# Key lookup in a product-key mixture: each chosen index picked on its token's partition by VectorE, or on the pair's partition by TensorE and VectorE

## The chip, the cores and the metric

One core of a Trainium2 chip runs the whole program. The metric is the device time of one execution in microseconds (us), lower is better. The core's engines run side by side and wait for each other through semaphores: TensorE (PE, with its weight loads shown as PEld), VectorE (DVE), ScalarE (ACT), GpSimd (POOL) and SyncE (SP), which issues DMAs. ACT issues DMAs too.

## What is computed

Two transformer blocks, one after the other, on 256 tokens of width 1024. The change lies in the last layer of the second block, a mixture of 16384 single-row experts with product keys:

```python
q = (xb @ w_q).reshape(TOK_BLOCK, PEER_HEADS, 2, PEER_DHALF)          # 256, 8, 2, 128
s = jnp.einsum('thcd,hcnd->thcn', q, sub_keys).astype(jnp.float32)    # 128 scores per list
top_s, top_i = lax.top_k(s, K)                                        # K = 16
cand = top_s[:, :, 0, :, None] + top_s[:, :, 1, None, :]
best_s, best_c = lax.top_k(cand.reshape(TOK_BLOCK, PEER_HEADS, K * K), K)
i1 = jnp.take_along_axis(top_i[:, :, 0], best_c // K, axis=-1)
i2 = jnp.take_along_axis(top_i[:, :, 1], best_c % K, axis=-1)
e = (i1 * PEER_NKEYS + i2).reshape(TOK_BLOCK, PEER_HEADS * K)
gate = jax.nn.softmax(best_s, axis=-1).reshape(TOK_BLOCK, PEER_HEADS * K)
act = jax.nn.gelu(jnp.einsum('td,ted->te', xb, expert_u[e]), approximate=False)
return jnp.einsum('te,ted->td', gate * act, expert_v[e])
```

So every token has 8 heads with two lists of 128 scores. The 16 best of each list are kept, all 256 sums of a pair of lists are formed, the 16 best sums are kept, and each names a place in the first list (its number divided by 16) and one in the second (the remainder). `i1` and `i2` are the keys found at these places.

## The kernel before

**The expert layer as matrix products.** The kernel does not gather expert rows. It forms the activations of all 16384 experts, in 128 chunks of 128, and multiplies them by a dense matrix `G` of gates, which is zero where an expert was not chosen. `act(c)` (line 1887) takes one chunk of `expert_u`: 24 matmuls of 128x256 in float32 parts (each number is a high part plus a low part, three products of eight slices of the width), then a Gelu on ACT (line 1893). The first 90 chunks run before `G` is needed and are parked in DRAM (line 1908).

**The weight stream.** Chunks come through class `Stream`: SP loads a raw chunk (4 buffers), ACT rounds it to the high part (line 362), and DVE or POOL subtracts to get the low part (line 363). Three buffers `hl` hold split chunks, so a chunk can be split only when the one three places ahead of it has been multiplied. Line 658 gives the subtraction to POOL for chunks below `POOLU` (36), and to DVE for the others.

**The choice beside it.** `queries` (line 1717) makes the 16 projections `qT` on PE, splits them (ACT high part, DVE low part), splits the keys `kT` and scores them. `choose` (line 1762) is a generator on DVE: `top16` (line 1751) is five operations (MAX8, FIND_INDEX8, MATCH_REPLACE8, MAX8, FIND_INDEX8) and runs for 16 lists in each of two token tiles, on 128 tokens as partitions. Then for each tile and head one addition makes the 256 sums `cand` (line 1780) and `top16` finds the best of them, values `bv` and numbers `bi`. Line 1786 and 1787 cut `bi` into the two places. The lookup compares each place with 0 to 15 (`eq`, line 1794), multiplies by the list's indices `tf` (line 1796) and sums over the 16 (line 1799): for each tile, side and head two operations of 128x256, so 32 comparisons and 32 products, and 4 sums. After that come the softmax, PE transposes (line 382) that put the 128 pairs (8 heads x 16) on partitions, and copies to `gi` (indices) and `gg` (the gates as a sum of three bf16 numbers, through `left`, lines 1824 to 1829).

**The gates.** `gates` (line 1832) makes 64 groups of four tokens: DVE one-hot tiles `e` and `m`, 12 bf16 matmuls of 128x128 on PE, a copy into `G` by ACT.

**What sets the order.** `first` (line 1905) writes `act(c)`, then takes as many steps of the side generator (`choose`, then `gates`) as its running sum allows: each step yields a number of ns, and the sum stays below `SIDE` (2850) times the chunks so far. Nine steps of `choose` are taken inside `queries`. A scheduler then places instructions on each engine. In `queries` it keeps the written order on DVE and in the first loop of `first` on ACT, but it may still bring other instructions forward into them.

Names: `hl_9657` is a buffer's tile with its number; `pb` are the PSUM tiles of `act` and `queries` (4), `py` those of the side work (4), `raw` the loaded chunks.

Of the kernel before, what the change touches and what calls it, by code (L numbers as in the profile page):

```python
# [29 lines left out]
WP = 400  # L30
EXP_M05 = math.exp(-0.5)
C0 = 90
POOLU = 36
LENT = 3
OUT = 1000
QUAD, PAIR = 150, 20
# [9 lines left out]
SIDE = 2850  # L46
LATE, CH = 6000, 1.0
# [11 lines left out]
def bias_onehot(dist):  # L59
# [6 lines left out]
CONST = {}  # L66
CONST_GROUPS = [["ident"], ["flip", "hpar", "hpair", "maskc"],
                ["mean512", "blk64", "strict", "incl", "lev1", "lev2", "lev4", "lev8", "lev16", "eye32", "ind", "indt"],
                ["iota"]]


def make_consts():
    p = np.arange(128)
    parts = {}
# [2 lines left out]
    parts["mean512"] = np.full((128, 128), 1.0 / 512)  # L77
    parts["blk64"] = (p // 64)[:, None] == (p // 64)[None, :]
    parts["iota"] = np.tile(np.arange(128), (128, 1))
    s64, t64 = (p % 64)[:, None], np.arange(64)[None, :]  # L80
    parts["strict"] = s64 < t64
    parts["incl"] = s64 <= t64
# [258 lines left out]
class Kern:  # L341
# [1419 lines left out]

    def choose(self, tk, sc, gi, gg):

        nc = self.nc
        found = []
        best = [(tk.tile([128, 16, 16], F32, name=f"tv{tt}"), tk.tile([128, 16, 16], U32, name=f"ti{tt}")) for tt in range(2)]
        for g in range(4):
            for tt in range(2):
                for k in range(4 * g, 4 * g + 4):
                    self.top16(tk, sc[tt][:, k], best[tt][0][:, k], best[tt][1][:, k])  # L1770
                    yield 1700 * CH
        for tt in range(2):
            tv, ti = best[tt]
            tf = tk.tile([128, 16, 16], F32, tag="tf", name=self.name("tf"), bufs=1)
            nc.vector.tensor_copy(tf, ti)
            bv = tk.tile([128, 8, 16], F32, tag="bv", name=self.name("bv"), bufs=1)
            bi = tk.tile([128, 8, 16], U32, tag="bi", name=self.name("bi"), bufs=1)
            for h in range(8):
                cand = tk.tile([128, 16, 16], F32, tag="cand", name=self.name("cand"), bufs=2)
                nc.vector.tensor_add(cand, tv[:, 2 * h, :, None].to_broadcast([128, 16, 16]),  # L1780
                                     tv[:, 2 * h + 1, None, :].to_broadcast([128, 16, 16]))
                self.top16(tk, cand.rearrange("p a b -> p (a b)"), bv[:, h], bi[:, h])
                yield 2900 * CH
            rs = []
            ij = [tk.tile([128, 8, 16], U32, tag=f"ij{c}", name=self.name("ij"), bufs=1) for c in range(2)]
            nc.vector.tensor_scalar(ij[0], bi, 4, None, op0=OP.logical_shift_right)
            nc.vector.tensor_scalar(ij[1], bi, 15, None, op0=OP.bitwise_and)
            for c in range(2):
                jf = tk.tile([128, 8, 16], F32, tag="jf", name=self.name("jf"), bufs=2)
                nc.vector.tensor_copy(jf, ij[c])  # L1790
                eq = tk.tile([128, 8, 16, 16], F32, tag="eq", name=self.name("eq"), bufs=1)
                res = tk.tile([128, 8, 16], F32, tag="res", name=self.name("res"), bufs=4)
                for h in range(8):
                    nc.vector.tensor_tensor(eq[:, h], jf[:, h, :, None].to_broadcast([128, 16, 16]),
                                            self.iota[:, None, :16].to_broadcast([128, 16, 16]), op=OP.is_equal)
                    nc.vector.tensor_mul(eq[:, h], eq[:, h], tf[:, 2 * h + c, None, :].to_broadcast([128, 16, 16]))
                    if h % 4 == 3:
                        yield 3400 * CH
                nc.vector.tensor_reduce(res, eq, axis=AX.X, op=OP.add)
                rs.append(res)  # L1800
                yield 2400 * CH
            ev = tk.tile([128, 8, 16], F32, tag="ev", name=self.name("ev"), bufs=2)
            nc.vector.tensor_sub(ev, bv, bv[:, :, 0:1].to_broadcast([128, 8, 16]))
            found.append((rs, ev))
        yield LATE
        sm = tk.tile([128, 2, 8], F32, name="smx")
        for tt, (_, ev) in enumerate(found):
            nc.scalar.activation(ev, ev, AF.Exp)
            nc.vector.tensor_reduce(sm[:, tt], ev, axis=AX.X, op=OP.add)
        nc.vector.reciprocal(sm, sm)  # L1810
        for tt, (_, ev) in enumerate(found):
            nc.vector.tensor_mul(ev, ev, sm[:, tt, :, None].to_broadcast([128, 8, 16]))
        yield 2 * SIDE
        for tt, (rs, ev) in enumerate(found):
            t = slice(tt * 32, tt * 32 + 32)
            p = self.pb()
            for c, x in enumerate((*rs, ev)):
                self.tr(p[:, c * 128:(c + 1) * 128], x.rearrange("p a b -> p (a b)"))
            nc.scalar.activation(gi[:, t].rearrange("p b c t -> p c b t"),
                                 p[:, :256].rearrange("p (c b t) -> p c b t", c=2, t=4), AF.Copy)  # L1820

            part = gg[:, t].rearrange("p b k t -> p k b t")
            src = p[:, 256:384].rearrange("p (b t) -> p b t", t=4)
            for k in range(3):
                nc.scalar.activation(part[:, k], src, AF.Copy)
                if k < 2:
                    left = tk.tile([128, 32, 4], F32, tag="left", name=self.name("left"), bufs=2)
                    nc.vector.tensor_sub(left, src, part[:, k])
                    src = left
        yield 600  # L1830

    def gates(self, gp, G, gi, gg):
# [26 lines left out]
    def peer(self, ctx):  # L1859
        tc, nc, A = self.tc, self.nc, self.A  # L1860
        st = self.st
        pp = ctx.enter_context(tc.tile_pool(name="peer", bufs=1))
        self.wide = ctx.enter_context(tc.tile_pool(name="wide2", bufs=1, space=PSUM))
        self.consts(3, pp)
        self.iota = self.c("iota")
        hT = self.hT
        self.iota2 = pp.tile([128, 128, 2], BF16, name="iota2")
        nc.gpsimd.tensor_copy(self.iota2, self.iota[:, :, None].to_broadcast([128, 128, 2]))
# [4 lines left out]
        tk = tke.enter_context(tc.tile_pool(name="topk", bufs=1))  # L1873
        sc = [tk.tile([128, 16, 128], F32, name=f"sc{tt}") for tt in range(2)]
        choose = self.choose(tk, sc, gi, gg)
        with tc.manual_schedule(engines={mybir.EngineType.DVE}):
            self.queries(tk, hT, sc, choose)
# [40 lines left out]
        with tc.manual_schedule(engines={mybir.EngineType.Activation}):  # L1918
            c = first(0, lambda c: self.G is not None or c == C0)
# [96 lines left out]
```

## Time and profile before

| | |
|---|---|
| three runs | 1550.85, 1552.71, 1559.87 us; median 1552.71 |
| the profiled execution | 1557.66 us, of which its span is 1555.9 us |
| PE busy | 1450.3 us, 93% of the span |
| DVE busy | 1135.2 us, 73% |
| ACT busy | 805.4 us, 52% |
| POOL busy | 271.3 us, 17% |
| expert layer | from about 690 us to the end; first loop from 747 us, `gates` from 930 to 1079 us |

Times within the profile count from the span's start. The clock of TensorE stands in the windows as a share of full speed: 1.00 is 2.4 GHz and 0.50 is 1.2 GHz. An idle time is named by what ended it.

### The profile page before, as it was taken

How to read it: one execution, taken by the hardware profiler on the slowest of the kernel's cores; microseconds unless marked ns; L12 is line 12 of the kernel's file. 1: busy time of each engine (PE TensorE's matmuls, PEld its weight loads, DVE VectorE, ACT ScalarE, POOL GpSimd, SP SyncE). 2: the span in 40 equal slices, each digit the busy share in tenths (PEclk: the TensorE clock that was granted, in tenths of full speed). 3: DMA queues.
4: the chain of work that ended last, by engine and by line, in shares of the span. 5: the costliest groups of instructions: out<-in, count | busy, mean ns of one | idle time of the engine just before them, and what ended most of it. 6: DMA issues, size and time to landing. Idle time of an engine off the chain costs nothing. (4 is left out here: it accounts for less than half of the span.)

```text
span 1555.9 us, 29408 instructions
## 1 busy us (share of the span) xinstructions
PE 1450.3 (93%) x11816; PEld 1321.3 (85%) x11816; DVE 1135.2 (73%) x2036; ACT 805.4 (52%) x1274; POOL 271.3 (17%) x136
## 2 busy tenths in 40 slices
PE   5999999998988789999998399999999999999997
PEld 4989799997877679989998399999999998888886
DVE  6765776778579974957999759987555556776776
ACT  4634565555463445544544167776444445455444
POOL 3100310004353323035786000000000000000000
PEclk9999999999899989999999699999999999999999
DMA  6622455554422211454565274444555557777773
GB/s 212 235 87 82 135 189 179 186 189 168 137 95 84 70 61 69 165 175 160 182 231 197 78 223 150 154 165 164 191 188 187 189 190 253 254 241 242 241 243 129
DMA packets 93024, 263.43 MB, mean 169 GB/s; under 512 B 10271, under 2 KB 34975, under 8 KB 92760
## 3 DMA queue, kind: packets, MB, share of 16 engines
q1 hardware_dynamic: 77200, 243.80, 46.4%
q10 hardware_dynamic: 15688, 17.76, 3.2%
q8 instruction: 92, 1.51, 0.4%
q14 instruction: 44, 0.36, 0.1%
HBM read 247.61 MB, written 13.91 MB: 168 GB/s over the span
## 5 line engine op out<-in xcount | busy, mean ns | idle before, releaser
L370 PE MATMUL pb<-hT,hl 128*128 128x256 f32 (+1 forms) x4944 | 629.6, 286 | 33.9 <-DVE hl L363 30.4
L370 PEld LDWEIGHTS pb<-hT,hl 128*128 128x128 f32 x4944 | 612.7, 193 | 41.4 <-DVE hl L363 30.8
L362 ACT ACTIVATE hl<-raw 128x1024 fp32r<-128x1024 f32 x412 | 434.3, 1054 | 236.9 <-issue 161.4
L363 DVE TENSOR_TENSOR hl<-raw,hl 128x1024 fp32r<-128x1024 f32 (+1 forms) x319 | 391.7, 1229 | 116.6 <-ACT hl L362 116.3
L370 PE MATMUL py<-hl,coef 128*128 128x512 f32 x1536 | 356.8, 390 | 0.8 <-ACT coef L362 0.6
L370 PEld LDWEIGHTS py<-hl,coef 128*128 128x128 f32 x1536 | 285.5, 188 | 60.6 <-ACT coef L362 1.4
L363 POOL TENSOR_TENSOR hl<-raw,hl 128x1024 fp32r<-128x1024 f32 x93 | 229.8, 2475 | 343.1 <-ACT hl L362 227.8
L1893 ACT ACTIVATE act<-pb 128x256 f32<-128x256 f32 x128 | 49.5, 387 | 179.5 <-PE pb L370 179.5
L1972 POOL TENSOR_TENSOR end<-end,end 128x512 f32<-128x512 f32 x2 | 2.6, 1278 | 700.5 <-DVE end L1970 699.0
L370 PE MATMUL py<-hT,hl 128*128 128x272 f32 (+1 forms) x768 | 118.0, 304 | 1.6 <-POOL hl L363 1.6
L370 PEld LDWEIGHTS py<-hT,hl 128*128 128x128 f32 x768 | 103.1, 198 | 8.3 <-issue 4.8
L363 DVE TENSOR_TENSOR coef<-act,coef 128x256 fp32r<-128x256 f32 x128 | 54.1, 423 | 72.4 <-ACT coef L362 72.4
L1897 DVE TENSOR_TENSOR act<-act,G 128x256 f32<-128x256 f32 x128 | 53.8, 421 | 35.4 <-ACT act L1893 33.2
L1246 DVE SCALAR_TENSOR_TENSOR acc<-UU,vt,acc 128x256 f32<-128x256 f32 x120 | 75.7, 673 | 0.7
L1856 ACT ACTIVATE G<-py 128x512 f32<-128x512 f32 x64 | 67.9, 1132 | 8.0 <-PE py L370 7.9
L1843 DVE TENSOR_TENSOR m<-e,gg 128x1536 bf16<-128x1536 bf16 x64 | 60.7, 954 | 0.8
L370 PE MATMUL py<-m,e 128*128 128x128 bf16 x768 | 53.6, 219 | 1.0 <-DVE m L1843 0.8
L362 ACT ACTIVATE coef<-act 128x256 fp32r<-128x256 f32 x128 | 51.6, 404 | 4.5 <-DVE act L1897 4.5
L1839 DVE TENSOR_TENSOR e<-gi,iota 128x1024 bf16<-128x1024 bf16 x64 | 43.6, 687 | 8.8 <-PE py L370 8.7
L370 PEld LDWEIGHTS <-e 128*128 128x128 bf16 x768 | 44.3, 97 | 5.6 <-DVE m L1843 3.0
L370 PE MATMUL py<-hl,gu 128*128 128x512 f32 x192 | 47.4, 393 | 0.3 <-DVE hl L363 0.2
L370 PEld LDWEIGHTS py<-hl,gu 128*128 128x128 f32 x192 | 34.9, 188 | 7.6 <-DVE hl L363 0.5
(408 smaller groups left out, 1424.6 us busy)
## 6 DMA issues: line engine op xcount, KB each, us to landing
raw<-in_ws_dram SPq DMA_DIRECT2D x172, 512.0 KB, 3.4
raw<-in_ut_dram SPq DMA_DIRECT2D x128, 512.0 KB, 3.3
raw<-in_ev_dram SPq DMA_DIRECT2D x128, 512.0 KB, 4.2
ad<-act ACTq DMA_DIRECT2D x90, 128.0 KB, 3.1
act<-ad SPq DMA_DIRECT2D x90, 128.0 KB, 3.1
wf<-fd ACTq DMA_DIRECT2D x2, 800.0 KB, 4.6
x<-in_x_dram SPq DMA_DIRECT2D x2, 512.0 KB, 5.9
xd<-x ACTq DMA_DIRECT2D x1, 1024.0 KB, 4.1
```

The lines of the kernel that those rows point to most:

```text
L362: self.nc.scalar.activation(h, src, AF.Copy)
L363: (eng or self.nc.vector).tensor_sub(l, src, h.bitcast(F32))
L370: self.nc.tensor.matmul(out, lhsT, rhs, start=start, stop=stop, skip_group_check=True)
L1246: nc.vector.scalar_tensor_tensor(acc[:, i], UU[:, i, 16 + j:272 + j], self.v("cw", 4 * j + i), acc[:, i], op0=OP.mult, op1=OP.add)
L1839: nc.vector.tensor_tensor(e.rearrange("p c a i j -> p (c a) i j"), gi[:, b].rearrange("p c (a j) -> p (c a) j", j=2)[:, :, None, :].to_bro ...
L1843: nc.vector.tensor_mul(m, e[:, 0][:, None].to_broadcast([128, 3, 2, 128, 2]), gg[:, b].rearrange("p k (a j) -> p k a j", j=2)[:, :, :, Non ...
L1856: nc.scalar.activation(G[:, :, 4 * b:4 * b + 4].rearrange("p a t -> p t a"), p.rearrange("p (t a) -> p t a", t=4), AF.Copy)
L1893: nc.scalar.activation(a, p[:, :S], AF.Gelu)
L1897: nc.vector.tensor_mul(a, a, self.G[:, c])
L1972: nc.gpsimd.tensor_mul(t[:, tt], x[:, tt, cols[1]], g[:, cols[1]])
```

## The change

It replaces the comparisons, products and sums of the lookup. The places are transposed to pairs on partitions as numbers (`pT`, two sides, 256 tokens), and so are the lists of indices (`tT`, bf16). `sel` is a constant set of 16 matrices, made once from `cst3`: matrix r has a one where row h*16+r meets the 16 columns of head h. `spread` multiplies it with `tT`: each pair's partition receives the index that stands at place r of its head's list. One DVE operation compares the places with r and multiplies with that (`hit`, bf16), and a matmul with the identity (`identb`) adds it into `found`; with r from 0 to 15 and two sides these are 32 spreading matmuls, 32 DVE operations and 32 adding matmuls, all 128x256. The sums `cand` of eight heads become one operation of 128x2048 per tile. Casts go to ACT (`tf`, `pf`). The yields are new, `POOLU` is 38, and `cst3` moves from the pool `peer` to the pool `topk`.

```diff
-POOLU = 36
+POOLU = 38
-                ["iota"]]
+                ["iota", "place"]]
+    parts["place"] = p[:, None] - p[None, :] // 16 * 16
     def choose(self, tk, sc, gi, gg):
...
-                    yield 1700 * CH
+                    yield 1650 * CH
+        bv = [tk.tile([128, 8, 16], F32, name=f"bv{tt}") for tt in range(2)]
+        bi = [tk.tile([128, 8, 16], U32, name=f"bi{tt}") for tt in range(2)]
         for tt in range(2):
...
+            cand = tk.tile([128, 8, 16, 16], F32, tag="cand", name=self.name("cand"), bufs=1)
+            nc.vector.tensor_add(cand, tv[:, 0::2, :, None].to_broadcast([128, 8, 16, 16]),
+                                 tv[:, 1::2, None, :].to_broadcast([128, 8, 16, 16]))
+            yield 2300 * CH
             for h in range(8):
...
-                yield 2900 * CH
...
+                self.top16(tk, cand[:, h].rearrange("p a b -> p (a b)"), bv[tt][:, h], bi[tt][:, h])
+                yield 2400 * CH
+        ev, pl, tf = [], [], []
+        for tt in range(2):
+            x = tk.tile([128, 8, 16], F32, name=f"ev{tt}")
+            nc.vector.tensor_sub(x, bv[tt], bv[tt][:, :, 0:1].to_broadcast([128, 8, 16]))
+            ev.append(x)
+            x = tk.tile([128, 2, 128], U32, name=f"place{tt}")
+            flat_bi = bi[tt].rearrange("p a b -> p (a b)")
+            nc.vector.tensor_scalar(x[:, 0], flat_bi, 4, None, op0=OP.logical_shift_right)
+            nc.vector.tensor_scalar(x[:, 1], flat_bi, 15, None, op0=OP.bitwise_and)
+            pl.append(x)
+            yield 900 * CH
         yield LATE
         sm = tk.tile([128, 2, 8], F32, name="smx")
+        pf = []
+        for tt in range(2):
+            x = tk.tile([128, 2, 8, 16], F32, name=f"tf{tt}")
+            nc.scalar.activation(x.rearrange("p c h r -> p h c r"), best[tt][1].rearrange("p (h c) r -> p h c r", c=2), AF.Copy)
+            tf.append(x)
+            x = tk.tile([128, 2, 128], F32, name=f"pf{tt}")
+            nc.scalar.activation(x, pl[tt], AF.Copy)
+            pf.append(x)
+            nc.scalar.activation(ev[tt], ev[tt], AF.Exp)
...
+        identb = tk.tile([128, 128], BF16, name="identb")
+        nc.scalar.activation(identb, self.ident, AF.Copy)
...
-        yield 2 * SIDE
+        yield SIDE
+        pT = tk.tile([128, 2, 256], F32, name="pT")
+        tT = tk.tile([128, 2, 256], BF16, name="tT")
+        for tt in range(2):
+            p = self.p1()
+            for c in range(2):
+                self.tr(p[:, c * 128:(c + 1) * 128], tf[tt][:, c].rearrange("p h r -> p (h r)"))
+            nc.scalar.activation(tT[:, :, tt * 128:tt * 128 + 128], p[:, :256].rearrange("p (c t) -> p c t", c=2), AF.Copy)
+            p = self.p1()
+            for c, x in enumerate((pf[tt][:, 0], pf[tt][:, 1], ev[tt].rearrange("p a b -> p (a b)"))):
+                self.tr(p[:, c * 128:(c + 1) * 128], x)
+            nc.scalar.activation(pT[:, :, tt * 128:tt * 128 + 128], p[:, :256].rearrange("p (c t) -> p c t", c=2), AF.Copy)
...
+            yield 900
+        found = self.p1()
+
+        def spread(c, r):
+            p = self.p1()
+            for i in range(2):
+                self.mm(p[:, 256 * i:256 * i + 256], self.sel[:, r + i], tT[:, c], True, True)
+            return p
+
+        todo = [(c, r) for c in range(2) for r in range(0, 16, 2)]
+        nxt = spread(*todo[0])
+        for n, (c, r) in enumerate(todo):
+            p = nxt
+            if n + 1 < len(todo):
+                nxt = spread(*todo[n + 1])
+            for i in range(2):
+                w = tk.tile([128, 256], BF16, tag="hit", name=self.name("hit"), bufs=3)
+                nc.vector.scalar_tensor_tensor(w, pT[:, c], float(r + i), p[:, 256 * i:256 * i + 256], op0=OP.is_equal, op1=OP.mult)
+                self.mm(found[:, 256 * c:256 * c + 256], identb, w, r + i == 0, r + i == 15)
+            yield 950 * CH
+        nc.scalar.activation(gi.rearrange("p b c t -> p c b t"), found.rearrange("p (c b t) -> p c b t", c=2, t=4), AF.Copy)
         yield 600
     def peer(self, ctx):
...
-        self.consts(3, pp)
...
+        self.consts(3, tk)
...
+        self.sel = tk.tile([128, 16, 128], BF16, name="sel")
+        nc.vector.tensor_tensor(self.sel, self.c("place")[:, None, :].to_broadcast([128, 16, 128]),
+                                self.c("iota")[:, :16, None].to_broadcast([128, 16, 128]), op=OP.is_equal)
```

Lines after the change stand one lower at first (the split is lines 363 and 364, `act` is line 1922). What the schedule makes of it is shown at three places.

First DVE where `queries` begins, before the change: the low part of a chunk, then the low parts of the queries (`qT`) and of the keys (`kT`).

```order
L363 TENSOR_TENSOR hl_7710<-raw_7416,hl_7710 128x1024
L363 TENSOR_TENSOR qT<-pb_7705,qT 128x256 x2
L363 TENSOR_TENSOR qT<-pb_7750,qT 128x256 x2
L363 TENSOR_TENSOR qT<-pb_7725,qT 128x256
L363 TENSOR_TENSOR qT<-pb_7801,qT 128x256
```

The same place after the change:

```order
L364 TENSOR_TENSOR hl_7710<-raw_7416,hl_7710 128x1024
L1902 TENSOR_TENSOR sel<-cst_7775 128x2048
L364 TENSOR_TENSOR qT<-pb_7705,qT 128x256 x2
L364 TENSOR_TENSOR qT<-pb_7750,qT 128x256 x2
L364 TENSOR_TENSOR qT<-pb_7725,qT 128x256
```

`sel` now stands ahead of the first query. On ACT's queue the DMA of `cst3` moved from ahead of six splits and copies to just ahead of the DMA of the keys (`kr`).

Second, DVE between two projections inside `queries`, before the change: an operation of the first `top16` steps, then the sums of one head, brought forward from later, and the start of their `top16`.

```order
L1760 MAX_INDEX ti_7925<-tv_7924,s_880_7966 128x8
L1780 TENSOR_TENSOR cand_8933<-tv_7924 128x256
L1756 MAX bv_8931<-cand_8933 128x8
L1757 MAX_INDEX bi_8932<-bv_8931,cand_8933 128x8
L1758 MATCH_REPLACE s_998_8935<-bv_8931,cand_8933 128x256
L363 TENSOR_TENSOR qT<-pb_7977,qT 128x256
L363 TENSOR_TENSOR kT<-kr,kT 128x512
```

The same place after the change:

```order
L1760 MAX tv_7926<-s_880_7968 128x8
L1761 MAX_INDEX ti_7927<-tv_7926,s_880_7968 128x8
L364 TENSOR_TENSOR qT<-pb_7979,qT 128x256
L364 TENSOR_TENSOR kT<-kr,kT 128x512
L1757 MAX tv_7926<-sc_7778 128x8
```

The head's sums no longer stand there; a second head's, 27 rows on, are gone in the same way.

Third, ACT after the change, where the lookup begins: `act_9687` is chunk 32, `hl_9737` is the split of chunk 35 and `hl_9797` that of chunk 36.

```order
L1937 DMA ad<-act_9687 128x256
L1820 ACTIVATE tT<-py_9692 128x2x128
L1824 ACTIVATE pT<-py_9696 128x2x128
L1830 ACTIVATE gg<-py_9696 128x32x4
L1830 ACTIVATE gg<-left_9702 128x32x4
L1830 ACTIVATE gg<-left_9705 128x32x4
L1820 ACTIVATE tT<-py_9708 128x2x128
L1824 ACTIVATE pT<-py_9712 128x2x128
L1830 ACTIVATE gg<-py_9712 128x32x4
L1830 ACTIVATE gg<-left_9718 128x32x4
L1830 ACTIVATE gg<-left_9721 128x32x4
L363 ACTIVATE hl_9737<-raw_9543 128x1024
```

The split of chunk 35 stands behind ten copies, four of which wait for DVE. Before the change the corresponding copies stood between splits:

```order
L1819 ACTIVATE gi<-pb_10303 128x2x32x4
L1825 ACTIVATE gg<-pb_10303 128x32x4
L1893 ACTIVATE act_10442<-pb_10417 128x256
L362 ACTIVATE hl_10481<-raw_10228 128x1024
L1825 ACTIVATE gg<-left_10309 128x32x4
```

Two copies, a Gelu and a split stand there before the next copy that waits for DVE.

## Rows read from the trace of the kernel before

**Rows 1.** Who waited for whom, 690 to 1090 us: total us, times, longest.

```profile
PE pb L370 <- DVE hl L363: 29.7, 1, 29.7
...
PE pb L370 <- DVE qT L363: 3.2, 2, 1.9
```

**Rows 2.** Timeline of PE from 745 us: start, length, instructions [idle before <-releaser].

```profile
747.39 102.68 PE L370 MATMUL pb<-hT,hl 128*128 128x256 f32 x866
879.75 36.66 PE L370 MATMUL pb<-hT,hl 128*128 128x256 f32 x286 [29.68 <-DVE hl L363]
...
930.35 0.85 PE L370 MATMUL py<-m,e 128*128 128x128 bf16 x12
931.01 0.36 PE L370 MATMUL pb<-hT,hl 128*128 128x256 f32 x1
```

**Rows 3.** Windows: busy PE, PEld, DVE, ACT, POOL, then clock, DMA share, GB/s.

```profile
820.00:840.00 20.00, 20.00 (x172) 20.00 (x171) 20.00 (x16) 10.26 (x15) 17.62 (x8) 1.00 0.66 234
...
860.00:880.00 20.00, 0.25 (x1) 0.25 (x2) 19.83 (x51) 0.00 (x0) 0.00 (x0) 0.50 0.00 0
```

**Rows 4.** Groups by line, 700 to 930 us; columns: group, count | busy us, mean ns | idle before, releaser.

```profile
L363 POOL TENSOR_TENSOR hl<-raw,hl 128x1024 fp32r<-128x1024 f32 x45 | 110.8, 2463 | 36.5 <-ACT hl L362 36.5
L362 ACT ACTIVATE hl<-raw 128x1024 fp32r<-128x1024 f32 x63 | 66.7, 1059 | 21.5 <-ACT act L1893 21.0 <-DVE hl L363 0.5
L1794 DVE TENSOR_TENSOR eq<-jf,cst 128x256 f32<-128x256 f32 x32 | 29.7, 968 | 0.0
L1796 DVE TENSOR_TENSOR eq<-eq,tf 128x256 f32<-128x256 f32 x32 | 29.7, 968 | 0.0
...
L1780 DVE TENSOR_TENSOR cand<-tv 128x256 f32<-128x256 f32 x16 | 16.9, 1056 | 0.0
...
L1799 DVE TENSOR_REDUCE res<-eq 128x128 f32<-128x2048 f32 x4 | 9.1, 2277 | 0.1
...
L1893 ACT ACT_TABLE_LOAD x2 | 2.6, 1283 | 0.0
...
L1825 ACT ACTIVATE gg<-left 128x128 bf16<-128x128 f32 x4 | 1.2, 308 | 1.3 <-DVE left L1828 1.3
```

**Rows 5.** Timeline of DVE: two lookup pairs, and the end of the choice.

```profile
837.87 2.95 DVE L1794 TENSOR_TENSOR eq<-jf,cst 128x256 f32<-128x256 f32 x2
...
878.49 3.49 DVE L363 TENSOR_TENSOR hl<-raw,hl 128x1024 fp32r<-128x1024 f32 x3
```

**Rows 6.** Line 1794: ns min/median/max, first and last start, form.

```profile
L1794 DVE TENSOR_TENSOR eq<-jf,cst x32: 400/419/2649, 794.6 to 875.2; 128x256 f32<-128x256 f32 x32
```

**Rows 7.** Tile qT: the same columns.

```profile
L363 DVE TENSOR_TENSOR qT<-pb,qT x16: 403/420/426, 699.5 to 745.4; 128x256 fp32r<-128x256 f32 x16
```

**Rows 8.** Groups with shapes apart, whole span.

```profile
L1135 DVE SCALAR_TENSOR_TENSOR cv<-pb,vt,cv 128x254 f32<-128x254 f32 x44 | 21.0, 480 | 1.3
```

**Rows 9.** Timeline of PE, 675 to 745 us.

```profile
675.46 1.03 PE L382 MATMUL pb<-ident,xg 128*128 128x128 f32 x8
...
702.68 3.08 PE L370 MATMUL pb<-hT,hl 128*128 128x256 f32 x24 [1.30 <-DVE qT L363]
...
731.58 2.69 PE L370 MATMUL pb<-kT,qT 128*128 128x128 f32 x13 [1.86 <-DVE qT L363]
734.07 10.86 PE L370 MATMUL pb<-hT,hl 128*128 128x256 f32 x72
```

**Rows 10.** Windows of 2 us: busy PE, clock, DMA share, GB/s.

```profile
732.00:734.00 2.00, 2.00 (x12) 0.50 0.19 64
...
740.00:742.00 2.00, 2.00 (x19) 1.00 0.00 0
```

**Rows 11.** Timelines of ACT and POOL around the queries' start.

```profile
688.86 0.35 ACTq L689 DMA_DIRECT2D cst<-in_cst_dram  x1
...
698.63 0.35 ACTq L1721 DMA_DIRECT2D kr<-in_keys_dram  x1
...
690.76 0.40 POOL L1868 CAST iota<-cst 128x256 bf16<-128x256 f32 x1 [7.71 <-DMA cst<-in_cst_dram]
```

More of the change, by code (lines that the diff above doesn't have):

```diff
@@ L1764, in choose @@
         nc = self.nc
-        found = []
         best = [(tk.tile([128, 16, 16], F32, name=f"tv{tt}"), tk.tile([128, 16, 16], U32, name=f"ti{tt}")) for tt in range(2)]
@@ L1770, in choose @@
                     self.top16(tk, sc[tt][:, k], best[tt][0][:, k], best[tt][1][:, k])
-                    yield 1700 * CH
+                    yield 1650 * CH
+        bv = [tk.tile([128, 8, 16], F32, name=f"bv{tt}") for tt in range(2)]
+        bi = [tk.tile([128, 8, 16], U32, name=f"bi{tt}") for tt in range(2)]
         for tt in range(2):
-            tv, ti = best[tt]
-            tf = tk.tile([128, 16, 16], F32, tag="tf", name=self.name("tf"), bufs=1)
-            nc.vector.tensor_copy(tf, ti)
@@ L1776, in choose @@
-            bv = tk.tile([128, 8, 16], F32, tag="bv", name=self.name("bv"), bufs=1)
-            bi = tk.tile([128, 8, 16], U32, tag="bi", name=self.name("bi"), bufs=1)
-            for h in range(8):
[L1779 to L1782, printed above, removed]
-                yield 2900 * CH
@@ L1784, in choose @@
[L1784 to L1800, printed above, removed]
-                yield 2400 * CH
@@ L1802, in choose @@
-            ev = tk.tile([128, 8, 16], F32, tag="ev", name=self.name("ev"), bufs=2)
-            nc.vector.tensor_sub(ev, bv, bv[:, :, 0:1].to_broadcast([128, 8, 16]))
-            found.append((rs, ev))
+            tv, _ = best[tt]
+            cand = tk.tile([128, 8, 16, 16], F32, tag="cand", name=self.name("cand"), bufs=1)
+            nc.vector.tensor_add(cand, tv[:, 0::2, :, None].to_broadcast([128, 8, 16, 16]),
+                                 tv[:, 1::2, None, :].to_broadcast([128, 8, 16, 16]))
@@ L1805, in choose @@
         yield LATE
         sm = tk.tile([128, 2, 8], F32, name="smx")
-        for tt, (_, ev) in enumerate(found):
-            nc.scalar.activation(ev, ev, AF.Exp)
-            nc.vector.tensor_reduce(sm[:, tt], ev, axis=AX.X, op=OP.add)
-        nc.vector.reciprocal(sm, sm)
-        for tt, (_, ev) in enumerate(found):
-            nc.vector.tensor_mul(ev, ev, sm[:, tt, :, None].to_broadcast([128, 8, 16]))
-        yield 2 * SIDE
-        for tt, (rs, ev) in enumerate(found):
-            t = slice(tt * 32, tt * 32 + 32)
[L1816 to L1820, printed above, removed]
+        pf = []
@@ new lines, in choose @@
+        for tt in range(2):
[6 more added lines that the diff above has]
+            nc.scalar.activation(ev[tt], ev[tt], AF.Exp)
+            nc.vector.tensor_reduce(sm[:, tt], ev[tt], axis=AX.X, op=OP.add)
@@ new lines, in choose @@
+        identb = tk.tile([128, 128], BF16, name="identb")
+        nc.scalar.activation(identb, self.ident, AF.Copy)
+        nc.vector.reciprocal(sm, sm)
+        for tt in range(2):
+            nc.vector.tensor_mul(ev[tt], ev[tt], sm[:, tt, :, None].to_broadcast([128, 8, 16]))
+        yield SIDE
+        pT = tk.tile([128, 2, 256], F32, name="pT")
+        tT = tk.tile([128, 2, 256], BF16, name="tT")
+        for tt in range(2):
+            p = self.p1()
[6 more added lines that the diff above has]
+            nc.scalar.activation(pT[:, :, tt * 128:tt * 128 + 128], p[:, :256].rearrange("p (c t) -> p c t", c=2), AF.Copy)
+            t = slice(tt * 32, tt * 32 + 32)
@@ L1863, in peer @@
         self.wide = ctx.enter_context(tc.tile_pool(name="wide2", bufs=1, space=PSUM))
-        self.consts(3, pp)
-        self.iota = self.c("iota")
         hT = self.hT
         self.iota2 = pp.tile([128, 128, 2], BF16, name="iota2")
-        nc.gpsimd.tensor_copy(self.iota2, self.iota[:, :, None].to_broadcast([128, 128, 2]))
         gi = pp.tile([128, 64, 2, 4], BF16, name="gi")
@@ L1873, in peer @@
         tk = tke.enter_context(tc.tile_pool(name="topk", bufs=1))
+        self.consts(3, tk)
+        nc.gpsimd.tensor_copy(self.iota2, self.c("iota")[:, :, None].to_broadcast([128, 128, 2]))
         sc = [tk.tile([128, 16, 128], F32, name=f"sc{tt}") for tt in range(2)]
+        self.sel = tk.tile([128, 16, 128], BF16, name="sel")
+        nc.vector.tensor_tensor(self.sel, self.c("place")[:, None, :].to_broadcast([128, 16, 128]),
+                                self.c("iota")[:, :16, None].to_broadcast([128, 16, 128]), op=OP.is_equal)
         choose = self.choose(tk, sc, gi, gg)
```

## Prediction

> **What bounds the kernel now.** I read first who waited for whom in the expert layer, then the timeline of PE there, then the windows, and last the groups of DVE. PE is the busiest engine of the program, and in this layer it hardly pauses: 866 matmuls run without a break from 747.39 us for 102.68 us, 0.1186 us each [rows 2]. Then it stands still for 29.68 us, ended by the low part of a weight chunk on DVE [rows 1, 2]. Chunk 36 is the first whose low part DVE makes, and DVE has no time for it: it is full from 820 to 840 us beside a PE at full work, and full from 860 to 880 us beside a PE that does nothing [rows 3]. Its choice of keys ends only at 878.49 us, with the three low parts that PE needs right behind it [rows 5]. The 286 matmuls after the hole took 36.66 us, 2.75 us more than at 0.1186 us: the clock had fallen to 0.50, which is 1.2 GHz [rows 2, 3]. A smaller case of this stands in the queries: PE waits 1.86 us for a query's low part, and the 13 and 72 matmuls behind it take 13.55 us where 10.08 would do, at a clock of 0.50 that is back at 1.00 by 740 us [rows 9, 10].
>
> Outside these holes PE is the bound, so DVE's work counts only where it makes PE wait, and each matmul that is added counts in full.
>
> **What goes.** DVE loses the 32 comparisons and 32 products of 0.968 us mean, 59.4 us, four sums of 2.28 us, 9.1 us, and the sixteen `cand` additions, 16.9 us [rows 4]. The products and comparisons are so slow because DVE waits for POOL: a pair of them took 2.95 us while POOL was splitting, against a fastest single one of 0.40 us [rows 5, 6]. Two additions of 2048 elements take the place of sixteen. The row nearest to them is the sum over 2048 elements, 2.28 us, and a POOL operation of 2.46 us may stand in front of each [rows 4]; I take 3.5 us each, with bounds 2.3 and 4.8. So DVE's choice shrinks by 59.4 + 9.1 + 16.9 - 7.0 = 78 us and ends near 878.5 - 78 = 800 us. The yields ahead of `gates`, less the nine steps taken in the queries, were 23 x 1700 + 2 x (8 x 2900 + 18,400) + 12,300 = 134,600 ns; now they are 23 x 1650 + 2 x 21,500 + 1800 + 6000 + 2850 + 1800 + 16 x 950 + 600 = 109,200. At 2850 a chunk `gates` begins at chunk 38 instead of 47, and the written order puts the softmax behind chunk 31, near 747.4 + 32 x 2.85 = 838.5 us. DVE is 38 us early for it. What is late next is then the lookup itself, below.
>
> - The hole at 850 us goes, 29.68 us, and its slow matmuls, 2.75 us. It is covered by DVE's 78 us; 38 us of that are to spare.
> - The two heads' sums that stood inside the queries go, so the wait of 1.86 us and its 3.47 us of slow clock should go: 5.33 us.
>
> Together 37.8 us.
>
> **What comes.**
>
> - 64 bf16 matmuls of 256 columns. Twelve of 128 columns start 0.66 us before the next kind, 0.055 us each [rows 2], so 0.110 us for twice the columns and 7.0 us in all; bounds 0.055 (3.5 us) and 0.1186 (7.6 us). Nothing hides them. Four more transposes at 1.03 / 8 us are 0.5 us [rows 9].
> - `sel` stands on DVE ahead of the first queries. Its data now leave with the keys' DMA at 698.63 us instead of 688.86 [rows 11]. Before, 1.90 us passed from issue to use. That gives 700.5 us; a POOL split that may be in the way costs half its 2.46 us on average, the operation 2.28 us, and two low parts of 0.42 us [rows 7] follow before PE gets its buffer: 704.9 us. PE went on at 702.68 us [rows 9]. So 2.2 us; the wait then grows from 1.30 to 3.5 us, and I add one fall of the clock as in the queries, 3.5 us: 5.7 us. Bounds: nothing, if the data come early, and 8. ACT and POOL wait for none of this.
> - The wait at the lookup. Call the end of chunk 31 T. ACT must do 8 small operations (casts, Exp, Gelu) at about 0.31 us, a table load of 1.28 and a split of 1.06 before POOL can make chunk 34 in 2.46 us [rows 4]: T + 7.3. PE gets there at T + 2 x 2.85 + 10 x 0.13 = T + 7.0, and chunk 34 ends at T + 10.1. On ACT the split of chunk 35 stands behind ten copies, four of them fed by DVE, and one of those DVE operations stands behind the first two `hit` operations, which need the first spreading matmul. A `hit` reads one operand from PSUM; the nearest row is the 254-wide scalar_tensor_tensor with a PSUM operand, 0.48 us [rows 8]. So: T + 10.3, two hits to 11.3, the subtraction and its copy to 11.9, the split to 13.0, POOL to 15.4. PE has 16 lookup matmuls (1.8 us) to do from 10.1, then chunk 35 is not there: 3.5 us, and 0.3 us before chunk 34. Afterwards the 32 hits need 15.4 us of DVE, and PE has 7.0 us of lookup and three and a quarter chunks, 9.3 us, beside them: nearly even, with each of three batches waiting about one and a half hits (0.7 us): 2.1 us. Together 5.9 us, and one fall of the clock at the size of the first, 2.75 us: 8.7 us. Bounds: 1 us, if the copies come sooner, and 17, twice my value.
> - The longer `gates` with low parts on DVE is the same work, only ten chunks earlier; PE set its pace before and does so again. POOL's two more chunks need 2.46 us each against PE's 2.85, so it keeps up. SP issues the same DMAs in the same order; its waits are for buffers, which follow PE. I cost these at nothing; if POOL were late, 2 x 2.46 us.
>
> 7.0 + 0.5 + 5.7 + 8.7 = 21.9 us come, 37.8 us go: 15.9 us less. The profiled execution took 1557.66 us, so 1541.8. It stood 5 us above the median of the runs, 1552.71, and from that the forecast is 1537 us.
>
> The clock is the weakest term. The rows show a fall behind a wait of 1.86 us, and none behind the one of 1.30 us, where 24 matmuls followed in 3.08 us [rows 9, 10]; the one at the lookup is 3.5 us within some 5.3 us, so by them it costs 2.75 us. The Trainium skill, page "TensorE: Matmul & The Clock Gate", section "What's actually happening", says that the throttled clock is the default and that activity releases it. By that rule a lookup that keeps PE at work a third of the time might hold the clock up, and the sum would be 1534 us.
>
> **The rivals.**
>
> - The new waits are covered: the data of `sel` come in time, the copies are done sooner, no fall of the clock. Then 37.8 - 7.5 - 1 - 2 = 27.3 us go: 1525 us. For it: DVE and ACT have slack all along before the lookup, ACT half busy [rows 3]. Against it: the order on ACT, where the split stands behind all copies.
> - No change that can be measured. A `hit` costs what a comparison cost on average, 0.97 us [rows 4]: 32 x 0.49 = 15.7 us more, and the gain is gone: 1553 us. For it: POOL still splits chunks 35 to 37 during the lookup. Against it: DVE operations with an operand in PSUM took 0.403 to 0.426 us in the same stretch, with POOL at work [rows 7].
> - Slower. The `hit` operations pay the full price of the pairs under POOL, 2.95 / 2 = 1.47 us each [rows 5]: PE stands behind each, since an adding matmul follows every one in its queue. That is 32 x 0.99 = 31.7 us more than I count, 1569 us. It decides from 0.98 us per hit on, where the gain is used up. Against it: it needs POOL busy for all 32, and POOL has three chunks left, 7.4 us.
>
> The Trainium skill bears on these two, page "SBUF — State Buffer", section "Who interferes with whom": a VectorE instruction with at most one SBUF input does not contend with GpSimd, one with two does. By that a hit stays at 0.48 us and `sel` can be held up. The trace agrees: 0.403 to 0.426 us with PSUM, up to 2.649 us without [rows 6, 7]. The two rivals keep a small chance.
>
> **How the numbers follow.** One per cent, 15.5 us, is about what a measurement of this kernel can tell from no change. The forecast has 0.60, and since it lies at that bound I split it: 0.33 above 1% and 0.27 below. The covered case has 0.20, all faster. No change has 0.13, slower 0.07. So faster 0.53, same 0.40, slower 0.07. The forecast's own range, with both clock falls gone or one more of them, and the bounds of the lookup, is 1529 to 1545 us. The range that holds 8 in 10 reaches toward the covered case and toward no change: 1523 to 1549 us.
>
> **What would show it.** Right: no wait of PE for DVE's low parts near 850 us; DVE's choice done near 800 us; `gates` beginning at chunk 38; no hole at 731 us; a wait of 2 to 4 us near 702 and one near 850, each with a stretch at clock 0.50; hits near 0.48 us. Wrong: hits above 0.7 us; a hole of over 5 us in the lookup; DVE's choice ending later than 838 us, for then ACT waits for it and the splits stand behind; or a `gates` stage that is longer than its 149 us.

## The result, and the profile after

| | before | after |
|---|---|---|
| median of the runs | 1554.60 us (1550.85 to 1559.87) | 1538.97 us (1531.44 to 1540.11) |
| ratio | 1 | 0.9887, interval 0.9842 to 0.9932 |
| profiled execution | 1557.66 us, span 1555.9 | 1540.11 us, span 1538.4 |
| first query projection to first chunk | 695.01 to 747.39: 52.38 us | 698.37 to 751.42: 53.05 us |
| first chunk to first coefficient matmul | 747.39 to 1092.89: 345.50 us | 751.42 to 1076.32: 324.90 us |

The kernel became 15.6 us faster by the medians. In the profiled executions the expert layer lost 19.9 us up to its first coefficient matmul (397.88 against 377.95 us), and the changed kernel reached the layer 3.4 us later. In the profiles of this study that point lies anywhere from 692.87 to 701.96 us, for both kernels and in no order with the edits; what moves it stays open. So stages are compared below by their length.

The waits in the expert layer of the changed kernel, from 690 to 1090 us (total, times, longest), which answer to [rows 1]:

```profile
DVE smx L1807 <- ACT ev L1806: 38.5, 2, 38.0
...
DVE sel L1902 <- DMA cst<-in_cst_dram: 9.0, 1, 9.0
DVE hit L1852 <- PE py L371: 5.7, 5, 1.7
...
PE pb L371 <- DVE qT L364: 5.2, 1, 5.2
...
PE pb L371 <- POOL hl L364: 2.5, 3, 1.5
```

The 29.7 us for DVE's low parts are not in the list any more. PE waits 5.2 us at the queries and 2.5 us in all for POOL's splits, and DVE now stands idle for 38 us. PE's timeline shows where (start, length, instructions, idle before); it answers to [rows 2, 9]:

```profile
698.37 3.09 PE L371 MATMUL pb<-hT,hl 128*128 128x256 f32 x24
...
709.96 8.25 PE L371 MATMUL pb<-hT,hl 128*128 128x256 f32 x48 [5.22 <-DVE qT L364]
...
720.68 5.89 PE L371 MATMUL pb<-hT,hl 128*128 128x256 f32 x48
...
775.26 71.37 PE L371 MATMUL pb<-hT,hl 128*128 128x256 f32 x598 [0.68 <-POOL hl L364]
846.47 0.38 PE L383 MATMUL py<-ident,tf 128*128 128x128 f32 x2
...
854.16 0.61 PE L371 MATMUL py<-tT,sel 128*128 128x256 bf16 x4
855.06 0.27 PE L371 MATMUL py<-hit,identb 128*128 128x256 bf16 x1 [0.29 <-DVE hit L1852]
...
859.32 0.50 PE L371 MATMUL pb<-hT,hl 128*128 128x256 f32 x2 [1.48 <-POOL hl L364]
...
881.01 0.85 PE L371 MATMUL py<-m,e 128*128 128x128 bf16 x12
```

Two places are to be seen. At 709.96 us stands the new wait for `sel`, and the 48 matmuls behind it take 8.25 us where the next 48 take 5.89. From 854 to 874 us lies the lookup, with no wait above 1.48 us. The windows of 2 us (busy PE, PEld, DVE, ACT, POOL, then clock, DMA share, GB/s), which answer to [rows 3, 10], give the clock at both:

```profile
710.00:712.00 2.00, 2.00 (x9) 2.00 (x10) 1.44 (x5) 1.71 (x4) 1.19 (x1) 0.50 0.00 0
...
716.00:718.00 2.00, 2.00 (x19) 2.00 (x18) 0.24 (x1) 0.73 (x1) 1.19 (x1) 1.00 0.00 0
...
858.00:860.00 2.00, 0.68 (x5) 0.61 (x6) 0.32 (x2) 1.54 (x3) 2.00 (x2) 1.00 0.28 99
860.00:862.00 2.00, 2.00 (x19) 1.78 (x16) 1.96 (x6) 0.41 (x1) 2.00 (x2) 1.00 0.90 268
```

The clock fell to 0.50 (1.2 GHz) behind the wait for `sel` and did not fall in the lookup, not even where PE was busy for 0.68 of 2 us. The timelines of ACT, POOL and DVE show the causes; they answer to [rows 5, 11]:

```profile
702.01 0.35 ACTq L690 DMA_DIRECT2D cst<-in_cst_dram  x1
702.39 0.54 ACTq L1722 DMA_DIRECT2D kr<-in_keys_dram  x1
...
706.40 2.46 POOL L1898 CAST iota<-cst 128x256 bf16<-128x256 f32 x1 [1.32 <-DMA cst<-in_cst_dram]
...
706.32 2.29 DVE L1902 TENSOR_TENSOR sel<-cst 128x2048 bf16<-128x2048 f32 x1 [8.98 <-DMA cst<-in_cst_dram]
708.52 0.41 DVE L364 TENSOR_TENSOR qT<-pb,qT 128x256 fp32r<-128x256 f32 x1
...
806.55 2.01 DVE L1793 TENSOR_SCALAR place<-bi 128x128 uint32<-128x128 uint32 x1
...
808.82 0.21 DVE L1793 TENSOR_SCALAR place<-bi 128x128 uint32<-128x128 uint32 x1
846.99 0.29 DVE L1807 TENSOR_REDUCE smx<-ev 128x8 f32<-128x128 f32 x1 [37.95 <-ACT ev L1806]
...
855.46 2.85 DVE L1852 SCALAR_TENSOR_TENSOR hit<-pT,py 128x256 bf16<-128x256 f32 x8
859.99 2.30 DVE L1852 SCALAR_TENSOR_TENSOR hit<-pT,py 128x256 bf16<-128x256 f32 x6 [1.68 <-PE py L371]
```

`sel` started 4.31 us after its data were issued, and the first low part of a query stood behind it. DVE's choice ended at 808.82 us, and its next operation came 38 us later. The groups from 700 to 930 us answer to [rows 4]:

```profile
L1852 DVE SCALAR_TENSOR_TENSOR hit<-pT,py 128x256 bf16<-128x256 f32 x32 | 11.6, 415 | 5.7 <-PE py L371 5.7
...
L371 PE MATMUL py<-hit,identb 128*128 128x256 bf16 x32 | 8.4, 277 | 0.4 <-DVE hit L1852 0.3
...
L371 PE MATMUL py<-tT,sel 128*128 128x256 bf16 x32 | 5.9, 274 | 0.0
L1779 DVE TENSOR_TENSOR cand<-tv 128x2048 f32<-128x2048 f32 x2 | 4.9, 2440 | 0.0
```

In place of 85.4 us for comparisons, products, `cand` and the sums over 16 [rows 4] DVE has 11.6 us of hits and 4.9 us for `cand`.

### The profile page after: what moved, and what is told of

It is laid out like the page before. It is cut to its first block, busy times and chain, and to the rows that moved or that the text cites. A ratio compares the mean times of both kernels' runs of the same rounds, so it can differ in the third digit from the quotient of the medians.

```text
span 1538.4 us, 29510 instructions
## 1 busy us (share of the span) xinstructions
PE 1455.4 (95%) x11884; PEld 1325.3 (86%) x11884; DVE 1067.6 (69%) x1979; ACT 807.3 (52%) x1282; POOL 280.9 (18%) x138
## 4 chain that ended last, share of the span: by engine, by line
PE 75%; DVE 16%; ACT 4%; DMA 2%; issue 2%; POOL 1%; SPq 0%; ACTq 0%; DVEq 0%; POOLq 0%
PE pb L371 39%; PE py L371 35%; DVE acc L1247 4%; DVE hl L364 2%; ACT hl L363 1%; PE pb L383 1%; DMA raw<-in_ws_dram 1%; POOL hl L364 1%; DVE m L1869 1%; DVE nc L425 0%; DMA x<-in_x_dram 0%; DVE blk L736 0%; ACT junk L515 0%; DVE nc L426 0%; DMA cst<-in_cst_dram 0%
## 5 line engine op out<-in xcount | busy, mean ns | idle before, releaser
L364 POOL TENSOR_TENSOR hl<-raw,hl 128x1024 fp32r<-128x1024 f32 x95 | 236.8, 2499 | 354.7 <-ACT hl L363 234.1
```

The costliest lines, as they stand in the source:

```text
L364: (eng or self.nc.vector).tensor_sub(l, src, h.bitcast(F32))
```

## The experiments

The theory: the hole went because DVE's choice became short enough to end before the splits need DVE; what was paid for it is the wait for `sel` with the clock behind it, and the lookup's own matmuls. The rivals: the two chunks more on GpSimd did it, or the joined candidate sums did, or the added matmuls lie beside other work.

**`sel` built behind the queries.** The changed kernel with one operation moved:

```
     def queries(...):
         ...
+        nc.vector.tensor_tensor(self.sel, self.c("place")[...], self.c("iota")[...], op=OP.is_equal)
     def peer(...):
         ...
-        nc.vector.tensor_tensor(self.sel, self.c("place")[...], self.c("iota")[...], op=OP.is_equal)
         choose = self.choose(tk, sc, gi, gg)
```

> The changed kernel with one edit: the constant sel is made at the end of the queries instead of ahead of them. Theory (sel costs what the profile shows at the start: a wait of 5.2 us for a query's low part, 3.9 us longer than before, and 2.6 us of slow clock behind it): the wait near 706 us falls back to 1.3 to 2.2 us, the clock stays at 1.00 through the queries, and the time falls by 5 to 7 us, to a ratio of 0.983 to 0.986 with before. Rival (the queries wait for the keys' data or for ACT anyway, sel only stands in front): the wait stays over 4 us and the time within 2 us of the changed kernel's.

Measured: 1534.33 us, ratio 0.9856 (0.9824 to 0.9888). PE's timeline of this kernel:

```profile
696.02 3.09 PE L371 MATMUL pb<-hT,hl 128*128 128x256 f32 x24
...
703.68 3.08 PE L371 MATMUL pb<-hT,hl 128*128 128x256 f32 x24 [1.30 <-DVE qT L364]
707.76 3.08 PE L371 MATMUL pb<-hT,hl 128*128 128x256 f32 x24 [0.99 <-DVE qT L364]
...
744.05 94.68 PE L371 MATMUL pb<-hT,hl 128*128 128x256 f32 x792
```

From the first projection to the first chunk it takes 48.03 us, 5.0 less than the changed kernel. The waits are 1.30 and 0.99 us in place of 5.22, and 24 matmuls at full clock take 3.08 us behind each. `sel` itself took 3.43 us on DVE, at 744.14 us, and no PE wait lies there. The theory of this term holds, though the medians differ by 4.6 us where 5 to 7 were expected. The interval overlaps the changed kernel's, so the runs alone do not separate the two; but the two kernels that build `sel` late have medians of 1534.33 and (last experiment) 1533.72 us, and the four that build it at the start 1538.49 to 1541.70. Both late ones are faster than the kernel before beyond doubt. How much they gain on the changed one is read from the profiles alone: the two take 48.03 and 48.43 us from the first projection to the first chunk, and the three kernels with the same queries that build `sel` at the start take 53.05, 52.50 and 50.71 us. So the price of `sel` there is 2.3 to 5.0 us, by how late its data land.

**GpSimd's two chunks alone.** The kernel before with

```
-POOLU = 36
+POOLU = 38
```

> The kernel before with POOLU 38 alone. Theory (the gain is DVE's relief): the hole only moves by two chunks; DVE's choice ends near 882 us, since two more POOL splits slow some of its comparisons, PE comes to chunk 38 at 856 us, and the hole is 24 to 28 us; the time is within 3 us of before, ratio 0.998 to 1.002. Rival (the limit of POOL is what made the kernel faster): the hole is under 15 us and the ratio 0.99 to 0.993.

Measured: 1558.17 us, ratio 1.0002 (0.9980 to 1.0024). PE's timeline:

```profile
714.72 4.39 PE L370 MATMUL pb<-hT,hl 128*128 128x256 f32 x24 [3.04 <-DVE qT L363]
...
890.70 30.40 PE L370 MATMUL pb<-hT,hl 128*128 128x256 f32 x238 [24.88 <-DVE hl L363]
```

The hole is still 24.88 us. Two chunks on POOL move its start by two chunks and leave its end where it was (133.2 us behind the first chunk, against 132.4); the rival falls. The queries took 56.51 us here, 4.1 more than in the profile before, with a wait of 3.04 us that stands nowhere in it: the keys' data landed 8.7 us after their issue, against 5.8. The edit does not touch the queries, so their length can differ by some 4 us from one execution to another.

**The joined sums alone.** The kernel before with the candidate sums of eight heads in one operation:

```
+            cand = tk.tile([128, 8, 16, 16], F32, tag="cand", ...)
+            nc.vector.tensor_add(cand, tv[:, 0::2, :, None]..., tv[:, 1::2, None, :]...)
+            yield 2300 * CH
             for h in range(8):
-                cand = tk.tile([128, 16, 16], F32, tag="cand", ...)
-                nc.vector.tensor_add(cand, tv[:, 2 * h, :, None]..., tv[:, 2 * h + 1, None, :]...)
-                self.top16(tk, cand..., bv[:, h], bi[:, h])
-                yield 2900 * CH
+                self.top16(tk, cand[:, h]..., bv[:, h], bi[:, h])
+                yield 2400 * CH
```

> The kernel before with the candidate sums of eight heads in one operation, the lookup unchanged, yields of the sums as in the change. Theory (the hole's end is the end of DVE's choice): DVE loses 10 us of sums, so PE goes on at about 870 us instead of 879.75; the wait of 1.86 us in the queries goes too, but its 5.3 us only make PE arrive earlier at the hole; the time falls by 8 to 12 us, ratio 0.992 to 0.995. Rival (the sums are most of the gain): ratio 0.990 or less. Second rival (the lookup is all of it): ratio 0.998 to 1.002.

Measured: 1555.29 us, ratio 0.9977 (0.9956 to 0.9999), less than the gain expected and next to the second rival's range. The groups of DVE from 700 to 900 us, and PE's hole:

```profile
L1795 DVE TENSOR_TENSOR eq<-jf,cst 128x256 f32<-128x256 f32 x32 | 32.0, 1039 | 0.0
...
L1779 DVE TENSOR_TENSOR cand<-tv 128x2048 f32<-128x2048 f32 x2 | 7.2, 3594 | 0.0
...
L1788 DVE TENSOR_SCALAR ij<-bi 128x128 uint32<-128x128 uint32 x2 | 2.7, 1328 | 0.0
L1787 DVE TENSOR_SCALAR ij<-bi 128x128 uint32<-128x128 uint32 x2 | 2.6, 1320 | 0.0
```

```profile
884.53 20.64 PE L370 MATMUL pb<-hT,hl 128*128 128x256 f32 x154 [30.43 <-DVE hl L363]
```

The queries took 48.52 us, 3.9 less than before, without the wait of 1.86 us. But the hole ended 182.6 us after the first projection, against 184.7 us: the expected 10 us at the end of the choice came to 2.2. The sums did shrink from 16.9 us [rows 4] to 7.2. Of the 9.7 us, DVE stood idle for 3.3 more while it waited for the queries (18.7 us against 15.4 in the first 58 us from the first projection), the comparisons took 2.3 us more (32.0 against 29.7), and the two cuts of `bi` 4.5 us more (5.3 against 0.8), partly given back by the casts behind them (0.7 against 2.9). In all DVE was busy 5.6 us less up to the end of the hole. So a part of what DVE saved early was lost again, in waits and in operations that now met POOL's splits. And since PE comes 2.9 us earlier to its hole, the hole is longer, not shorter. So in the kernel before the joined sums are worth about 2 us: what the queries gain goes into the hole.

**The lookup alone.** The changed kernel with one sum per head, as before, and the yield of 2900 with it (the diff above, turned around).

> The changed kernel with the sums of one head in one operation as before (yield 2900 for each head), the lookup new. Theory (DVE is 38 us early for the softmax, so 10 us more of sums cost nothing there): no hole after the queries; in the queries two heads' sums stand between the projections again, and the wait of 1.9 us with 3.5 us of slow clock may come back: 0 to 6 us more than the changed kernel, ratio 0.989 to 0.993. Rival (the sums make a part of the gain by themselves at the end of the choice): 10 us more or above, ratio 0.995 and up.

Measured: 1541.70 us, ratio 0.9876 (0.9830 to 0.9923). PE's timeline:

```profile
739.98 1.67 PE L371 MATMUL pb<-kT,qT 128*128 128x128 f32 x13 [1.86 <-DVE qT L364]
741.49 10.24 PE L371 MATMUL pb<-hT,hl 128*128 128x256 f32 x72
...
754.54 5.74 PE L371 MATMUL pb<-hT,hl 128*128 128x256 f32 x47
```

The queries' wait of 1.86 us is back with its slow matmuls, and the first chunk starts 56.59 us behind the first projection, 3.5 us more than in the changed kernel; no hole follows at the end of the choice. The ratio lies below the expected range; the medians, taken at different times, are 2.7 us apart, inside the expected 0 to 6. The runs alone do not tell the two kernels apart. From the first projection to the first coefficient matmul it is 380.32 us, against 397.88 before and 377.95 in the changed kernel: the lookup carries 17.6 of the 19.9 us.

**The changed kernel without GpSimd's two chunks.** `POOLU` set back to 36.

> The changed kernel with GpSimd splitting the chunks up to 35 only, as the kernel before did, so that chunks 36 and 37 come to VectorE. Theory: VectorE stands idle for about 38 us before the softmax and its sums, products and hits for the first lookup fit between the spreading matmuls, so the choice ends early enough without GpSimd's two chunks; two more splits of 1.2 us each fall beside the hits on VectorE, and the lookup ends 0 to 2.5 us later: ratio 0.986 to 0.991 against the kernel before, no PE wait above 4 us between the first chunk and the coefficients. Rival: GpSimd's two chunks are what took the hole away; then TensorE waits for chunk 36's split 5 us or more behind the hits, and the ratio is 0.992 or more.

Measured: 1539.95 us, ratio 0.9890 (0.9846 to 0.9934). DVE's and PE's timelines:

```profile
860.55 1.22 DVE L364 TENSOR_TENSOR hl<-raw,hl 128x1024 fp32r<-128x1024 f32 x1
861.68 1.08 DVE L1852 SCALAR_TENSOR_TENSOR hit<-pT,py 128x256 bf16<-128x256 f32 x3
```

```profile
859.54 0.50 PE L371 MATMUL pb<-hT,hl 128*128 128x256 f32 x2 [1.48 <-POOL hl L364]
```

DVE makes the split of chunk 36 between hits, PE waits no longer than in the changed kernel, and from the first chunk to the first coefficient matmul it is 324.73 us against 324.90. So the two chunks on POOL do nothing that the profile shows here.

**Each spreading matmul twice.** The changed kernel with

```
             for i in range(2):
-                self.mm(p[...], self.sel[:, r + i], tT[:, c], True, True)
+                for _ in range(2):
+                    self.mm(p[...], self.sel[:, r + i], tT[:, c], True, True)
```

> The changed kernel with each of the 32 spreading matmuls issued twice (the same result). Theory: TensorE is the engine that the lookup's added matmuls lie on, each in full at 0.11 us at the full clock, so the 32 more add 3.5 us between chunk 31 and the gates, less what they fill of the waits that stand in the lookup (about 3.4 us idle over it, some of it between the spreading matmuls): 1 to 3.5 us more than the changed kernel, ratio 0.989 to 0.992. Rival: the lookup is paced by VectorE's hits (0.36 us each) and the ACT engine's and GpSimd's splits, and the added matmuls lie beside them: no change, ratio 0.986 to 0.989.

Measured: 1538.49 us, ratio 0.9884 (0.9840 to 0.9927). The windows from the first transpose to the first matmul of `gates`, first of the changed kernel, then of this one (busy PE, PEld, DVE, ACT, POOL, clock, DMA share, GB/s):

```profile
846.47:881.01 34.54, 32.25 (x261) 28.98 (x260) 20.67 (x49) 17.98 (x35) 9.40 (x4) 1.00 0.49 159
```

```profile
844.07:879.27 35.20, 34.77 (x292) 32.16 (x291) 20.68 (x49) 17.98 (x35) 9.43 (x4) 1.00 0.48 156
```

The stretch grew by 0.66 us, not by 3.5. PE's idle time in it fell from 2.29 to 0.43 us, and its busy time rose by 2.52. The rival is nearer: most of the added work filled gaps that the hits and splits leave, and isolated matmuls whose end had been waited for. In this stretch a bf16 matmul does not count in full. The median does not differ from the changed kernel's; the queries of this profile were 2.3 us shorter, more than the 0.66 us.

**The two tiles' copies apart.** The kernel of the first experiment with

```
-            yield 900
+            yield SIDE
```

behind the transposes of each tile, so that a chunk's split stands between the two rows of copies on ACT.

> The changed kernel with the selection matrix built behind the queries (as in the run before that had this alone, ratio 0.9856) and the step between the two tiles' transposes lengthened, so that a chunk's split stands between them on the ACT engine. Theory: TensorE's waits inside the lookup (0.68, 0.34 and 1.48 us for a split that stands behind the transposes' copies) come from ACT's row of copies; with the split between them the 1.48 us goes and no other wait above 1 us comes, 1 to 2.5 us less than with the matrix moved alone: ratio 0.984 to 0.985. Rival: the wait only moves (the second tile's copies come later, and the hits with them): no change, ratio 0.985 to 0.987.

Measured: 1533.72 us, ratio 0.9858 (0.9824 to 0.9892), no change against the first experiment. PE's timeline and the windows of 2 us:

```profile
840.77 3.26 PE L371 MATMUL pb<-hT,hl 128*128 128x256 f32 x24 [0.36 <-POOL hl L364]
845.95 0.66 PE L371 MATMUL pb<-hT,hl 128*128 128x256 f32 x2 [1.92 <-POOL hl L364]
```

```profile
844.00:846.00 2.00, 0.08 (x2) 0.05 (x1) 0.00 (x0) 0.83 (x3) 1.90 (x1) 1.00 0.19 66
846.00:848.00 2.00, 2.00 (x10) 1.63 (x11) 0.83 (x3) 0.17 (x1) 0.00 (x0) 0.53 0.52 162
848.00:850.00 2.00, 2.00 (x13) 1.67 (x13) 1.26 (x5) 1.45 (x4) 0.00 (x0) 0.61 0.26 104
```

The wait of 1.48 us among the hits became one of 1.92 us ahead of the first hit, and behind that one the clock fell, to 0.53 and 0.61 for 4 us. From the first chunk to the first coefficient matmul it is 325.63 us against 324.38 in the first experiment. The theory fell: the wait moved, and in this profile it cost the clock as well. (The wait of 0.68 us that the expectation counts to the lookup stands at 775.26 us in the changed kernel, 70 us ahead of it, and is not there in the first experiment.)

## Why the prediction came out right

The forecast was 1537 us and the runs gave 1538.97; 15.9 us less was the sum, 15.6 us less the difference of the medians. In the layer itself the profile shows 19.9 us less, 4.0 us more than the sum. That the sum and the medians agree to 0.3 us is luck in part: the terms below err by up to 4.4 us, and single executions of the kernel before lie between 1547.84 and 1564.57 us. The terms divide the profile's difference so:

| term | predicted | measured | from |
|---|---|---|---|
| hole and slow matmuls behind it | -32.4 us | gone whole | waits, PE's timeline |
| queries' wait and its clock | -5.3 us | -3.9 and -3.5 us | joined sums alone; lookup alone |
| `sel` at the start | +5.7 us | +5.0 us (2.3 to 5.0 over the profiles) | `sel` behind the queries |
| lookup: matmuls, waits, clock | +16.2 us | +11.8 us | 324.90 - (345.50 - 32.43) |

- **The mechanism was right.** DVE's choice ended 38 us ahead of the softmax. It did so 57.4 us behind the first chunk, where the prediction had 52.6 (800 less 747.4), although the sums cost 2.44 us each, less than the 3.5 taken. No term held what came in: DVE stood 8.98 us before the data of `sel`, and in the first 58 us from the first projection it was busy 36.40 us, 2.29 of them on `sel`, against 42.64 before; and one cut of `bi` cost 2.01 us under POOL. With 38 us to spare none of it mattered. GpSimd's two chunks alone and the joined sums alone leave the hole, and without either of them in the changed kernel none comes back, so the shorter lookup closes it. Its casts on ACT and its new yields stand in every one of these runs; none takes them apart from it.
- **The wait for `sel`.** Its size came out by two errors that met. The step "before, 1.90 us passed from issue to use" was taken over, and here 4.31 us passed: the profile lists the constants as 128 KB in place of 64, issued 0.38 us ahead of the keys' 1024 KB. Which of the two made them late was not tested; in the three other profiles that build `sel` at the start 2.77 to 3.64 us passed. So PE's wait was 5.22 us and not 3.5. The clock behind it cost 2.37 us (709.96 to 718.05 against 720.68 to 726.40), not 3.5.
- **The queries' wait.** The two rows of 1.86 us and slow matmuls were there to be gained, but PE waits elsewhere in its place: 1.30 and 0.99 us in the first experiment, against 1.30 alone near the start before [rows 9].
- **The lookup** is the term that was mis-sized, by 4.4 us. Its times on ACT and POOL came out well. With T at the end of chunk 31, 843.7 us (its Gelu starts at 843.82), the split of chunk 35 started on ACT at T + 12.1 (predicted 11.9) and PE resumed behind POOL at T + 15.6 (15.4). But the idle time was not one wait of 3.5 us. PE went on among hits until T + 14.1, so 1.48 us were left, and the three later batches waited for nothing worth a row where 2.1 us had been set. No clock fell, where 2.75 us had been set.
- **The clock** was called the weakest term, and it was. The traces hold both cases: where 3.5 us in one piece were foreseen, the waits came spread and the clock stayed at 1.00, and behind the 1.92 us in one piece of the last experiment it fell. The rule of the Trainium skill that activity releases the clock (page "TensorE: Matmul & The Clock Gate", section "What's actually happening") gave the better answer for this term, 0 us; the window of 0.68 us busy at 1.00 agrees with it.
- **The rivals.** A hit took 0.410 to 0.422 us, with POOL at 2.00 of 2 us in the window from 860; the rivals of 0.97 and 1.47 us fall. The Trainium skill, page "SBUF — State Buffer", section "Who interferes with whom", says that a VectorE instruction with one SBUF input, outside its two-port modes, does not contend with GpSimd, and the trace agrees for the hits. On `sel`, with two SBUF inputs, it agrees from the other side: POOL's cast beside it took 2.46 us against 0.40 [rows 11]. The covered case at 1525 us did not come either, since `sel` was late and the lookup cost more than its matmuls and 1 us.
- **How the lookup's 11.8 us divide** can be read from PE's busy time between the first chunk and the first coefficient matmul: 314.86 us before, 320.81 after. Less the 2.75 us of slow matmuls that went, PE works 8.7 us more, where 7.5 were set for matmuls and transposes. Its idle time there was 30.64 us, of which 29.68 were the hole, and is now 4.09: 3.1 us more, where 5.9 were set for waits and 2.75 for the clock. So the matmuls came out a little dearer than set, and the waits and the clock much cheaper. Busy time holds the modelled ends of single matmuls, though, and as the doubled spreading showed, an added matmul need not count in full in this stretch; how much of the 8.7 us is of that kind stays open.
- **A sign that misled.** A `gates` stage longer than its 149 us was to show the prediction wrong. It took 155.5 us (881.01 to 1036.48), against 148.3 before. But 896 matmuls of chunks ran within it in place of 825, and PE was idle for 0.97 us in it, against 0.93: the stage holds three chunks more and costs nothing for that.

## What to carry to other kernels

A hole of PE that a long chain on a second engine causes is closed by shortening the chain, and what is cut past the point where it is early enough buys nothing; then look for the next thing in that engine's queue, here a constant built where nobody needed it yet and the first query stood behind it. Take the landing time of a DMA from its new place and size, not from its old one. Where small gaps cannot be avoided, spread ones cost only themselves here; joined into one wait they cost PE the clock behind it as well, in the one profile that shows it.

## What was not expected of the hardware

- The clock behind PE's waits in the expert layer: 1.30, 1.39, 1.48 and, with the joined sums alone, 1.51 us were followed by matmuls at the full clock; behind 1.86, 1.92, 3.04 and 5.22 us it stood at 0.50 to 0.68 for a while. The longer wait did not cost more: behind the 1.86 us the slow matmuls took 3.47 us extra (13.55 against 10.08, as the prediction worked out from [rows 9]), behind the 5.22 us 2.37. The length alone does not settle it either. Near 185 us, in an earlier layer, PE waits in both kernels for an operation of DVE (`xg`) after a stretch at the full clock: behind 2.20 us of this wait the next 3 us stood at 1.00 in the first experiment, behind 2.24 us they stood at 0.50 with the joined sums alone.
- POOL's cast of `iota` took 2.46 us in every profile where `sel` ran on DVE at its side, and 0.40 or 0.41 us in the two kernels that build `sel` later.
- DVE operations with one input in SBUF, such as the cut of `bi`, were held up too where POOL was splitting: 2.01 us at 806.55 us, against 0.21 at 808.82. The prediction had used the rule on one SBUF input without its exception: the same section of the Trainium skill's page "SBUF — State Buffer" says that casts and `tensor_scalar` can, under conditions, run in a mode that uses two ports and then contend. The trace agrees for this cut; that the mode was the cause was not tested.
